# Three of four Strassen weight sums made by the DMA engines' adder on GpSimd's queue, and the pairs of a step in another order

## The chip, the cores and the metric

The kernel runs on one core of a Trainium2 chip. The metric is the device time of one execution in microseconds (us). Before the change it is 2227.79 us, the median of three runs (2227.02 to 2231.14). The engines named here are PE (TensorE, the matrix engine), DVE (VectorE), ACT (ScalarE), POOL (GpSimd) and SP (SyncE, which here only issues DMAs). The 16 DMA engines of the core are shared by all queues.

## The reference

One decoder layer on 256 tokens of width 2048, all in fp32. It holds two feed-forward layers (FFN), a mixer between them, and a per-layer embedding at the end:

```python
def swiglu(x, w_in, w_out):
    a, u = jnp.split(x @ w_in, 2, axis=-1)
    return (jax.nn.silu(a) * u) @ w_out

x = layer_norm(ALPHA * x + 0.5 * swiglu(x, ffn1_w_in[i], ffn1_w_out[i]), ln_g[i, 0], ln_b[i, 0])
...
x = layer_norm(ALPHA * x + merged @ mix_w_out[i], ln_g[i, 1], ln_b[i, 1])
x = layer_norm(ALPHA * x + 0.5 * swiglu(x, ffn2_w_in[i], ffn2_w_out[i]), ln_g[i, 2], ln_b[i, 2])
ple = jax.nn.sigmoid(x @ ple_w_gate[i]) * (p[i] @ ple_w_proj[i])
x = layer_norm(ALPHA * x + ple, ln_g[i, 3], ln_b[i, 3])
```

The hidden width D_FF is 5504. `x @ w_in` is the product that the change touches: it is [256, 2048] by [2048, 2 x 5504].

## The kernel before

**Passes.** To get nearly fp32 results from a faster matmul format, every operand is split into a high part (a cast) and a low part (operand less high part). A product of a 128-row block takes three matmuls of 128x128 by 128x512: high by high, high by low, low by high (L962, L963, L964).

**Weights.** Weights stream from HBM by SP's queue in pieces of two 128-row blocks by 512 columns (512 KB). ACT casts a piece to its high part `wh` (`weight_cast`, L897), DVE makes the low part `wl` (`weight_split`, L908). Such a piece, with what PE does with it, is called an element. Elements are used strictly in the order of the list `plan`. There are `NMAIN` = 6 slots for a `wh`/`wl` pair, so the cast of an element waits until PE has used up the one six places before it. Raw pieces have a ring of four buffers (`raw`); Strassen pieces have another ring of five (`sraw`).

**Strassen steps.** Chunks 2 to 10 of an FFN's columns are made by a `Quad`: the a half and the u half of a chunk, for both 128-token tiles, with part of the product done in Strassen's form. A Quad has two steps, and its pair of steps is followed by plain units on `w_out` (out units) for earlier chunks. There are nine Quads in each of two FFNs: 18 pairs, 36 steps. Each step loads four weight pieces k11, k12, k21, k22 into `sraw` and uses seven elements from them: 11, 22 and 21 as they are, and t1 to t4, which are sums. The sums are made in place, in the buffers that held the summands:

```python
"t1": dict(src=k11, add=k12, use=[("p5", "s1", lo)]),
"t3": dict(src=k12, add=k22, use=[("p7", "s3", lo)], free=[k12]),
"t2": dict(src=k11, add=k22, use=[("p6", "s2", lo)], drop=[k22]),
"t4": dict(src=k11, add=k21, use=[("p4", 1, hi)], drop=[k21], free=[k11]),
```

So t1, t2 and t4 follow one another in k11's buffer. `drop` gives a summand's buffer back after the sum, `free` gives the buffer back after the split; the pieces of the next step go into buffers so freed, in the order k12, k22, k21, k11. Four more elements (a0, a1, u0, u1) are plain raw pieces, each used for two products. The seven have one use (6 matmuls), the four have two (12 matmuls).

**What sets the order.** Whenever PE has used up an element, `feed` issues what it can, in this priority: a Strassen load, a raw load, a cast (with the sum in front of it on DVE, L891), a split. A scheduler then places the instructions of each engine in one fixed order, and inserts waits on semaphores; an engine runs its own list in order. The results of a Quad lie in seven PSUM banks p1 to p7; `after` combines them in the second step with DVE (L425) and ACT.

Of the kernel before, what the change touches and what calls it, by code (L numbers as in the profile page):

```python
# [14 lines left out]
ALU = mybir.AluOpType  # L15
# [15 lines left out]
LONG = (12, 4)  # L31
EXTRA = {"lead1": 3, "ffn1": 0, "tail1": 4, "hgrn": 0, "merge": 0, "lead2": 3, "ffn2": 0, "tail2": 4, "ple": 1}
NSRAW = 5
ALPHA = 2.0 ** 0.25
LN_EPS = 1e-5
RMS_EPS = 1e-6
# [30 lines left out]
class Quad:  # L67
# [11 lines left out]
    def __init__(self, stat, w, cols, width, after):  # L79
        self.stat, self.w, self.cols, self.width, self.after = stat, w, cols, width, after  # L80
        self.els = []
        for s in range(2):
            lo, hi = (2 * s, 2 * s + 1), (4 + 2 * s, 5 + 2 * s)
            n0, n1 = (8 + 4 * s, 9 + 4 * s), (10 + 4 * s, 11 + 4 * s)
            k11, k12, k21, k22 = ((self, s, n) for n in ("11", "12", "21", "22"))
            step = {
                "11": dict(src=k11, use=[("p1", 0, lo)]),
                "t1": dict(src=k11, add=k12, use=[("p5", "s1", lo)]),
                "22": dict(src=k22, use=[("p3", "s4", lo)]),
                "t3": dict(src=k12, add=k22, use=[("p7", "s3", lo)], free=[k12]),  # L90
                "t2": dict(src=k11, add=k22, use=[("p6", "s2", lo)], drop=[k22]),
                "21": dict(src=k21, use=[("p2", 0, hi)]),
                "t4": dict(src=k11, add=k21, use=[("p4", 1, hi)], drop=[k21], free=[k11]),
            }
            for n, ks in (("a0", n0), ("a1", n1)):
                step[n] = dict(load=[(ks, 0)], use=[("p2", 0, ks), ("p4", 1, ks)])
            for n, ks in (("u0", n0), ("u1", n1)):
                step[n] = dict(load=[(ks, 1)], use=[("p3", "d", ks), ("p5", 1, ks)])
            step["11"]["sums"] = [(k12, lo, 1), (k22, hi, 1), (k21, hi, 0), (k11, lo, 0)]
            order = "11 u0 t1 u1 22 t3 a0 t2 a1 21 t4".split()  # L100
            for n in order:
                self.els.append(dict(step[n], name=n, step=s))

# [2 lines left out]
def hybrid_layer(ctx: ExitStack, tc: tile.TileContext, x, p, ln_g, ln_b, ffn1_w_in, ffn1_w_out, mix_w_in,  # L106
                 conv_w, hg_lower_bound, hg_norm_w, branch_w_conv, branch_w_hgrn, mix_w_out,
                 ffn2_w_in, ffn2_w_out, ple_w_gate, ple_w_proj, out):
    nc = tc.nc
# [7 lines left out]
    op = pool("op", side="left")  # L117
# [111 lines left out]
    for b in (1, 2, 4, 8, 16, 32, 64):  # L229
        n = 64 // b  # L230
# [176 lines left out]
    def ffn(name, xs, w_in, w_out, ln_i, nxt):  # L407
        parts = [range(0, 2), range(2, 4), range(4, 6), range(6, 8), range(8, 11)]
        starts = [0, CC] + [DFF - (11 - ch) * CC for ch in range(2, 12)]
        gs = [Stat() for _ in parts]  # L410

        def turn(g, t, ci, h, w):
            defer(3, lambda: to_stat(g, t, ci, h, w // P, "g"))

        def in_units(ch, g, ci):
            c0 = starts[ch]
            w = starts[ch + 1] - c0
            if ch > 1:
                made = {}

                def work(tag):
                    return st.tile([P, CC], F32, tag=tag, name=tag, bufs=2 if tag == "silu" else 3)

                def both(o, a, b, op):
                    nc.vector.tensor_tensor(out=o, in0=a, in1=b, op=op)  # L425

                def after(el, ps):
                    if el["step"] == 0:
                        return
                    if el["name"] == "11":  # L430
                        made["c11"] = work("h")
                        nc.scalar.copy(made["c11"], ps["p1"])
                    elif el["name"] == "22":
                        made["c12"] = work("silu")
                        nc.scalar.copy(made["c12"], ps["p3"])
                        both(made["c12"], made["c12"], ps["p5"], ALU.add)
                    elif el["name"] == "t2":
                        made["e"], made["c22"] = work("silu"), work("h")
                        e = made["e"]
                        both(e, made["c11"], ps["p6"], ALU.add)  # L440
                        both(made["c12"], made["c12"], e, ALU.subtract)
                        both(e, e, ps["p7"], ALU.add)
                        both(made["c22"], ps["p5"], e, ALU.subtract)
                    elif el["name"] == "21":
                        h = made["c11"]
                        both(h, h, ps["p2"], ALU.add)
                        nc.scalar.activation(h, h, AF.Silu)
                        both(h, h, made["c12"], ALU.mult)
                        turn(g, 0, ci, h, CC)
                    elif el["name"] == "t4":  # L450
                        e = made["e"]
                        both(e, e, ps["p4"], ALU.add)
                        nc.scalar.activation(e, e, AF.Silu)
                        both(e, e, made["c22"], ALU.mult)
                        turn(g, 1, ci, e, CC)

                units.append(Quad(xs, w_in, (c0, DFF + c0), CC, after))
                return
            silu = {}

            def epi_a(t, acc):
                silu[t] = st.tile([P, CC], F32, tag="silu", name="silu", bufs=2)
                nc.scalar.activation(silu[t][:, :w], acc, AF.Silu)

            def epi_u(t, acc):
                h = st.tile([P, CC], F32, tag="h", name="h", bufs=3)
                nc.vector.tensor_tensor(out=h[:, :w], in0=silu[t][:, :w], in1=acc, op=ALU.mult)
                turn(g, t, ci, h, w)

            units.append(Unit(xs, w_in, 0, 16, c0, w, epi_a, split=(LONG if ln_i else EARLY) if ch == 0 else SPLIT))  # L470
            units.append(Unit(xs, w_in, 0, 16, DFF + c0, w, epi_u))

        def out_unit(pi, c):
            chunks, last = parts[pi], pi == len(parts) - 1
            row = starts[chunks[0]]
            nk = (starts[chunks[-1] + 1] - row) // P

            def epi_o(t, acc):
                settle(c)
                xc = xt[t][:, c * CC : (c + 1) * CC]  # L480
                if pi == 0:
                    nc.vector.scalar_tensor_tensor(out=xc, in0=xc, scalar=2.0 * ALPHA, in1=acc,
                                                   op0=ALU.mult, op1=ALU.add)
                else:
                    nc.vector.tensor_tensor(out=xc, in0=xc, in1=acc, op=ALU.add)
                if last:
                    ln_stat(t, c)
                    if c == 3:
                        layer_norm(t, ln_i, 0.5, nxt)

            units.append(Unit(gs[pi], w_out, row, nk, c * CC, CC, epi_o, split=(12,) if last and c == 3 else SPLIT))


        for pi, chunks in enumerate(parts):
            for ci, ch in enumerate(chunks):
                if ch == 1:
                    units.append(("ffn" + name, lambda: sums(xs)))
                in_units(ch, gs[pi], ci)
                if pi and ci < 2:
                    out_unit(pi - 1, 2 * ci)  # L500
                    out_unit(pi - 1, 2 * ci + 1)
        units.append(("tail" + name, lambda: None))
        for c in range(4):
            out_unit(len(parts) - 1, c)
# [325 lines left out]


    plan = []
    loads = {"raw": deque(), "sraw": deque()}
    for u in units:
        if isinstance(u, tuple):
            kind, n = u[0], EXTRA[u[0]]
            continue
        if isinstance(u, Quad):
            for el in u.els:
                for key, ks, n in el.get("sums", ()):  # L840
                    loads["sraw"].append((key, kind, u.w, ks[0] * P, 2, u.cols[n], u.width))
                if "load" in el:
# [35 lines left out]
    def drop(keys):  # L878
        for key in keys:
# [3 lines left out]
            else:  # L883
                held["freed"] += 1

    def weight_cast():
        el = plan[cur["cast"]]
        n, w, where = el["n"], el["w"], el["where"]
        raw = raws[el["src"]]
        if "add" in el:  # L890
            nc.vector.tensor_tensor(out=raw[:, :n, :w], in0=raw[:, :n, :w], in1=raws[el["add"]][:, :n, :w], op=ALU.add)  # L891
            drop(el.get("drop", ()))
        slots, bufs = (wp, NMAIN) if where == "main" else (region["pool"], EXTRA[where])
        h = slots.tile([P, KG, CC], F32R, tag="wh", name="wh", bufs=bufs)
        l = slots.tile([P, KG, CC], F32R, tag="wl", name="wl", bufs=bufs)
# [16 lines left out]
    def castable():  # L912
        i = cur["cast"]
        if i == len(plan) or i > cur["split"] + 1:
            return False
        el = plan[i]
        return (el["src"] in raws and el.get("add", el["src"]) in raws and room[el["where"]]
                and el["where"] in ("main", region["kind"]))

    def feed():  # L920
        while True:
            if may_load("sraw"):
                weight_dma("sraw")
            elif may_load("raw"):
                weight_dma()
            elif castable():
                weight_cast()
            elif cur["split"] < cur["cast"]:
# [119 lines left out]
```

## Time and profile before

| | before |
|---|---|
| median of 3 runs | 2227.79 us |
| the profiled execution | 2228.56 us |
| its span in the trace | 2226.7 us |
| granted PE clock, mean | 0.997 |
| read from HBM | 426.12 MB |

The profile is of one execution. Its page gives the busy time of each engine, the span in 40 slices, the DMA queues, the chain of work that ended last and the costliest groups of instructions. A group's row has the line of the kernel, engine, operation, the tiles written and read, their shape and the count, then the busy time in all and the mean in ns. A row of the timeline has start and duration in us, engine, line, operation, tiles and, in brackets, how long the engine had idled before it and what ended that. The rows themselves stand in the prediction, where they are used.

### The profile page before, as it was taken

Reading aid. Unit: us, or ns where it says so; the run is one execution under the profiler, and the core shown is the slowest. Engines: PE = TensorE matmul, PEld = TensorE weight load, DVE = VectorE, ACT = ScalarE, POOL = GpSimd, SP = SyncE. Lnnn points to the kernel's source line nnn. Section 1 sums busy time; section 2 is a strip of 40 time slices with the busy share of each in tenths; the row PEclk is TensorE's granted clock in tenths of the full one; section 3 lists DMA queues with packets and bytes.
Section 4 is the critical chain, followed back from the end, with each engine's and each line's share of the span. In section 5 each row is a group of like instructions: output and inputs, shape, how many; then the busy total and the mean of one; then the engine's idle time right before and its main releaser. Section 6 shows DMA issues by size and latency. Waiting matters only on the chain.

```text
span 2226.7 us, 26935 instructions
## 1 busy us (share of the span) xinstructions
PE 2203.0 (99%) x10110; PEld 1837.0 (82%) x10110; DVE 1685.6 (76%) x1952; ACT 1127.8 (51%) x1324; POOL 10.0 (0%) x32
## 2 busy tenths in 40 slices
PE   9999999999999999999999999999999999999997
PEld 7988888888887888888888888798888888888876
DVE  6788888888885678557555875769888888888668
ACT  5555555555555534434444443645555555555463
POOL 1000000000000000000000000000000000000000
PEclk9999999999999999999999999999999999999999
DMA  7666676566653665554555665567666556666564
GB/s 255 215 204 194 198 217 202 183 192 190 207 194 128 194 200 172 174 167 152 189 190 189 199 194 192 181 200 226 209 214 197 181 185 214 200 191 192 172 218 151
DMA packets 225334, 429.98 MB, mean 193 GB/s; under 512 B 13740, under 2 KB 22452, under 8 KB 225204
## 3 DMA queue, kind: packets, MB, share of 16 engines
q1 hardware_dynamic: 225204, 428.27, 60.6%
q8 instruction: 79, 1.29, 0.2%
q14 instruction: 51, 0.42, 0.1%
HBM read 426.12 MB, written 2.10 MB: 192 GB/s over the span
## 4 chain that ended last, share of the span: by engine, by line
PE 92%; DVE 4%; DMA 2%; ACT 1%; issue 1%; SPq 0%; DVEq 0%; ACTq 0%
PE bank L962 30%; PE bank L964 29%; PE bank L963 29%; DVE wl L908 2%; PE bank L243 2%; PE bank L600 1%; DVE sraw L891 1%; DMA raw<-in_ffn_w_in_dram 1%; ACT wh L897 0%; DMA sraw<-in_ffn_w_in_dram 0%; DMA gb<-in_ln_g_dram 0%; DMA x<-in_x_dram 0%; DMA raw<-in_ffn_w_out_dram 0%; DVE x L400 0%; DVE x L401 0%
## 5 line engine op out<-in xcount | busy, mean ns | idle before, releaser
L908 DVE TENSOR_TENSOR wl<-raw,wh 128x1024 fp32r<-128x1024 f32 (+2 forms) x660 | 788.6, 1203 | 262.8 <-ACT wh L897 245.4
L897 ACT CAST wh<-raw 128x1024 fp32r<-128x1024 f32 (+2 forms) x660 | 680.4, 1035 | 581.5 <-PE bank L964 410.1
L964 PE MATMUL bank<-wh,xl 128*128 128x512 f32 (+1 forms) x1736 | 670.9, 387 | 0.7 <-DVE xl L254 0.7
L963 PE MATMUL bank<-wl,xh 128*128 128x512 f32 (+1 forms) x1736 | 671.0, 387 | 0.0
L962 PE MATMUL bank<-wh,xh 128*128 128x512 f32 (+1 forms) x1736 | 669.6, 388 | 1.3 <-ACT xh L253 0.9
L897 ACT CAST wh<-sraw 128x1024 fp32r<-128x1024 f32 x252 | 262.5, 1050 | 273.1 <-PE bank L964 120.3
L908 DVE TENSOR_TENSOR wl<-sraw,wh 128x1024 fp32r<-128x1024 f32 x252 | 306.1, 1223 | 102.5 <-ACT wh L897 98.8
L964 PEld LDWEIGHTS bank<-wh,xl 128*128 128x128 f32 x1736 | 327.0, 188 | 64.5 <-DVE xl L254 2.4
L962 PEld LDWEIGHTS bank<-wh,xh 128*128 128x128 f32 x1736 | 327.1, 188 | 63.9 <-ACT xh L253 1.7
L963 PEld LDWEIGHTS bank<-wl,xh 128*128 128x128 f32 x1736 | 327.0, 188 | 61.8 <-DVE wl L908 0.2
L963 PE MATMUL bank<-wl,gh 128*128 128x512 f32 x880 | 343.9, 391 | 0.0
L964 PE MATMUL bank<-wh,gl 128*128 128x512 f32 x880 | 342.9, 391 | 0.0
L962 PE MATMUL bank<-wh,gh 128*128 128x512 f32 x880 | 341.9, 392 | 0.0
L964 PEld LDWEIGHTS bank<-wh,gl 128*128 128x128 f32 x880 | 165.4, 188 | 34.1
L962 PEld LDWEIGHTS bank<-wh,gh 128*128 128x128 f32 x880 | 165.3, 188 | 33.8
L963 PEld LDWEIGHTS bank<-wl,gh 128*128 128x128 f32 x880 | 165.4, 188 | 33.4
L891 DVE TENSOR_TENSOR sraw<-sraw 128x1024 f32<-128x1024 f32 x144 | 175.8, 1221 | 0.7
L964 PE MATMUL bank<-wh,sl 128*128 128x512 f32 x432 | 168.5, 390 | 0.0
L963 PE MATMUL bank<-wl,sh 128*128 128x512 f32 x432 | 168.4, 390 | 0.0
L962 PE MATMUL bank<-wh,sh 128*128 128x512 f32 x432 | 164.9, 390 | 0.5 <-ACT wh L897 0.5
L962 PEld LDWEIGHTS bank<-wh,sh 128*128 128x128 f32 x432 | 81.1, 188 | 17.9 <-ACT wh L897 1.4
L963 PEld LDWEIGHTS bank<-wl,sh 128*128 128x128 f32 x432 | 81.1, 188 | 16.9
(181 smaller groups left out, 1145.8 us busy)
## 6 DMA issues: line engine op xcount, KB each, us to landing
raw<-in_ffn_w_in_dram SPq DMA_DIRECT2D x176, 512.0 KB, 4.5
raw<-in_mix_w_in_dram SPq DMA_DIRECT2D x176, 512.0 KB, 4.6
raw<-in_ffn_w_out_dram SPq DMA_DIRECT2D x168, 512.0 KB, 4.9
sraw<-in_ffn_w_in_dram SPq DMA_DIRECT2D x144, 512.0 KB, 4.7
raw<-in_mix_w_out_dram SPq DMA_DIRECT2D x32, 512.0 KB, 5.4
raw<-in_ple_w_gate_dram SPq DMA_DIRECT2D x32, 512.0 KB, 4.9
raw<-in_ffn_w_in_dram SPq DMA_DIRECT2D x32, 384.0 KB, 4.0
raw<-in_branch_w_conv_dram SPq DMA_DIRECT2D x16, 512.0 KB, 4.9
```

Of the source, the lines that this page charges most:

```text
L243: state["turned"] = nc.tensor.transpose(tp[:, i * P : (i + 1) * P], src[:, i * P : (i + 1) * P], ident).ins
L600: nc.tensor.matmul(gp[:, (h * 2 + t) * 64 : (h * 2 + t + 1) * 64], kd[:, h, t * P : (t + 1) * P], qd[:, h, t, :], start=True, stop=True)
L891: nc.vector.tensor_tensor(out=raw[:, :n, :w], in0=raw[:, :n, :w], in1=raws[el["add"]][:, :n, :w], op=ALU.add)
L897: nc.scalar.copy(h[:, :n, :w], raw[:, :n, :w])
L908: nc.vector.tensor_tensor(out=l[:, :n, :w], in0=raw[:, :n, :w], in1=h[:, :n, :w].bitcast(F32), op=ALU.subtract)
L962: nc.tensor.matmul(acc, sh, wh[:, a, :n], start=first, stop=False)
L963: nc.tensor.matmul(acc, sh, wl[:, a, :n], start=False, stop=False)
L964: nc.tensor.matmul(acc, sl, wh[:, a, :n], start=False, stop=last)
```

## The change

The sums get a step of their own in `feed`, ahead of the cast. t1 stays on DVE. t2, t3 and t4 become DMAs with an adder, from one `sraw` buffer onto another, issued on GpSimd's queue. A sum is issued in the order of the list, when both summands are loaded and the split of an earlier element is issued (`behind`): of 11 for t1 and t3, of t1 for t2, of t2 for t4. The cast of a summed element now asks whether the sum has been issued. The order of a step's eleven elements changes, and two of the bank combinations in `after` hang on other elements.

```diff
+BY_DMA = ("t2", "t3", "t4")
...
-            order = "11 u0 t1 u1 22 t3 a0 t2 a1 21 t4".split()
+            order = "11 22 t1 21 u0 u1 t3 t2 a0 a1 t4".split()
+            for n, first in (("t1", "11"), ("t3", "11"), ("t2", "t1"), ("t4", "t2")):
+                step[n]["behind"] = len(order) * s + order.index(first)
...
-                    elif el["name"] == "22":
+                    elif el["name"] == "u1":
                         made["c12"] = work("silu")
...
-                    elif el["name"] == "21":
+                    elif el["name"] == "a1":
                         h = made["c11"]
...
+    def weight_add():
+        el = plan[adds.popleft()]
+        a, b = raws[el["src"]], raws[el["add"]]
+        if el["name"] in BY_DMA:
+            nc.gpsimd.dma_start(a, b, accum_op=ALU.add)
+        else:
+            nc.vector.tensor_tensor(out=a, in0=a, in1=b, op=ALU.add)
+        drop(el.get("drop", ()))
+        el["added"] = True
+
+    def addable():
+        if not adds:
+            return False
+        i = adds[0]
+        el = plan[i]
+        if el["src"] not in raws or el["add"] not in raws or cur["split"] <= el["behind"]:
+            return False
+        return el["name"] in BY_DMA or i <= cur["split"] + 1
...
     def weight_cast():
...
-        if "add" in el:
-            nc.vector.tensor_tensor(out=raw[:, :n, :w], in0=raw[:, :n, :w], in1=raws[el["add"]][:, :n, :w], op=ALU.add)
-            drop(el.get("drop", ()))
...
     def feed():
...
+            elif addable():
+                weight_add()
             elif castable():
```

What this does to DVE's list is seen at the start of a pair's second step. The number of an `sraw` tile tells which loaded piece it is. Before, 3447 is the second step's k11, 3117 its k12, 3375 its k22:

```order
L908 TENSOR_TENSOR wl_3459<-sraw_3447,wh_3458 128x1024 [waits DMAHW6_49,Activation_49]
L908 TENSOR_TENSOR wl_3475<-raw_3303,wh_3474 128x1024 [waits DMAHW0_49,Activation_49]
L891 TENSOR_TENSOR sraw_3447<-sraw_3447,sraw_3117 128x1024 [waits DVE_49]
L891 TENSOR_TENSOR sraw_3117<-sraw_3117,sraw_3375 128x1024 [waits DMAHW2_49,DVE_49]
L908 TENSOR_TENSOR wl_3488<-sraw_3447,wh_3487 128x1024 [waits Activation_49]
L908 TENSOR_TENSOR wl_3504<-raw_3352,wh_3503 128x1024 [waits DMAHW1_49,Activation_49]
L891 TENSOR_TENSOR sraw_3447<-sraw_3447,sraw_3375 128x1024 [waits DVE_49]
```

Now 3402 is the second step's k11, 3342 its k22, 3111 its k12, 3389 its k21 (a split is now L934, a sum on DVE L902):

```order
L934 TENSOR_TENSOR wl_3459<-sraw_3402,wh_3458 128x1024 [waits DMAHW6_49,Activation_49]
L934 TENSOR_TENSOR wl_3471<-sraw_3342,wh_3470 128x1024 [waits DMAHW1_49,Activation_49]
L902 TENSOR_TENSOR sraw_3402<-sraw_3402,sraw_3111 128x1024 [waits DVE_49]
L934 TENSOR_TENSOR wl_3481<-sraw_3402,wh_3480 128x1024 [waits Activation_49]
L934 TENSOR_TENSOR wl_3500<-sraw_3389,wh_3499 128x1024 [waits DMAHW3_49,Activation_49]
L934 TENSOR_TENSOR wl_3516<-raw_3364,wh_3515 128x1024 [waits DMAHW0_49,Activation_49]
L934 TENSOR_TENSOR wl_3528<-raw_3376,wh_3527 128x1024 [waits DMAHW2_49,Activation_49]
L934 TENSOR_TENSOR wl_3540<-sraw_3111,wh_3539 128x1024 [waits DMASW1_49,PE_49,Activation_49]
L934 TENSOR_TENSOR wl_3554<-sraw_3402,wh_3553 128x1024 [waits DMASW2_49,Activation_49]
```

Of the step's sums only t1 is left on DVE (36 in the whole program, where there were 144), and the splits of t3 and t2 (the last two rows) wait for semaphores of GpSimd's DMAs (DMASW).

POOL's list had nothing at this place. It now has the sums of all steps, one behind the other; 3069 and 3054 are the first step's k11 and k21:

```order
L900 DMA sraw_3069<-sraw_2996 128x1024 [waits DMASW5_49,DMASW0_49,DVE_49]
L900 DMA sraw_3069<-sraw_3054 128x1024 [waits DMAHW3_49,DMASW7_49,DVE_49]
L900 DMA sraw_3111<-sraw_3342 128x1024 [waits DMAHW7_49,DMAHW1_49,DVE_49]
L900 DMA sraw_3402<-sraw_3342 128x1024 [waits DMASW3_49,DMASW0_49,DVE_49]
L900 DMA sraw_3402<-sraw_3389 128x1024 [waits DMAHW3_49,DMASW2_49,DVE_49]
```

These are t2 and t4 of the first step, then t3, t2 and t4 of the second. Each t2 and t4 waits for the sum before it in the same buffer (DMASW) and for a split on DVE.

SP's list of loads at the same place, before:

```order
L868 DMA sraw_3375<-in_ffn1_w_in_dram 128x2x512 [waits DVE_49]
L868 DMA sraw_3406<-in_ffn1_w_in_dram 128x2x512 [waits DVE_49]
L868 DMA raw_3388<-in_ffn1_w_in_dram 128x2x512 [waits DMAHW6_49,DVE_49]
L868 DMA raw_3419<-in_ffn1_w_in_dram 128x2x512 [waits DMAHW7_49,DVE_49]
L868 DMA sraw_3447<-in_ffn1_w_in_dram 128x2x512 [waits DVE_49]
L868 DMA sraw_3450<-in_ffn1_w_in_dram 128x2x512 [waits DVE_49]
```

and now:

```order
L877 DMA sraw_3342<-in_ffn1_w_in_dram 128x2x512 [waits DMASW7_49,DMASW6_49]
L877 DMA raw_3376<-in_ffn1_w_in_dram 128x2x512 [waits DMAHW5_49,DVE_49]
L877 DMA sraw_3389<-in_ffn1_w_in_dram 128x2x512 [waits DVE_49]
L877 DMA raw_3414<-in_ffn1_w_in_dram 128x2x512 [waits DMAHW6_49,DVE_49]
L877 DMA raw_3426<-in_ffn1_w_in_dram 128x2x512 [waits DMAHW7_49,DVE_49]
L877 DMA sraw_3402<-in_ffn1_w_in_dram 128x2x512 [waits DMASW0_49]
L877 DMA sraw_3444<-in_ffn1_w_in_dram 128x2x512 [waits DVE_49]
```

Every Strassen load waited for DVE; now those of k22 (3342) and k11 (3402) wait for DMA sums of the step before, because these read or write the buffer that the load fills.

More of the change, by code (lines that the diff above doesn't have):

```diff
@@ L832, in hybrid_layer @@
     plan = []
+    adds = deque()
     loads = {"raw": deque(), "sraw": deque()}
@@ L838, in hybrid_layer @@
         if isinstance(u, Quad):
+            base = len(plan)
             for el in u.els:
+                if "add" in el:
+                    adds.append(len(plan))
+                    el["behind"] += base
                 for key, ks, n in el.get("sums", ()):
@@ L916, in castable @@
         el = plan[i]
-        return (el["src"] in raws and el.get("add", el["src"]) in raws and room[el["where"]]
+        return (el["src"] in raws and ("add" not in el or el.get("added")) and room[el["where"]]
                 and el["where"] in ("main", region["kind"]))
```

## The prediction

> **What bounds the kernel now.** I read the page's busy times first, then the slices, then who TensorE (PE) waits for, then single steps in the timeline.
>
> ```profile
> span 2226.7 us, 26935 instructions
> PE 2203.0 (99%) x10110; PEld 1837.0 (82%) x10110; DVE 1685.6 (76%) x1952; ACT 1127.8 (51%) x1324; POOL 10.0 (0%) x32
> PE   9999999999999999999999999999999999999997
> DVE  6788888888885678557555875769888888888668
> PEclk9999999999999999999999999999999999999999
> ```
>
> PE is busy for 99% of the span at full clock. VectorE (DVE) is at eight or nine tenths where the Strassen steps run (slices 2 to 12 and 26 to 36), but a high share is no bound by itself. A busy PE is also no proof that it runs at its own rate, so the waits come next, and then the distance between matmuls.
>
> ```profile
> PE bank L962 <- ACT wh L897: 0.5, 2, 0.3
> ...
> PEld bank L962 <- ACT wh L897: 1.4, 2, 0.7
> ...
> PEld bank L963 <- DVE wl L908: 0.2, 1, 0.2
> ...
> 289.06 0.39 PE L962 MATMUL bank<-wh,xh 128*128 128x512 f32 x1
> 289.29 0.39 PE L963 MATMUL bank<-wl,xh 128*128 128x512 f32 x1
> 289.51 0.39 PE L964 MATMUL bank<-wh,xl 128*128 128x512 f32 x1
> 289.74 0.39 PE L962 MATMUL bank<-wh,xh 128*128 128x512 f32 x1
> ```
>
> The first three rows (us in total, times, longest) are all of the waits for prepared weights in the whole run, PE's own and those of its weight loads: about 2 us. The starts in the timeline lie 0.227 us apart (289.74 less 289.06, by three), although one matmul is drawn 0.39 us long; they overlap. A step has 7 elements with one use and 4 with two, so 7 x 6 + 4 x 12 = 90 matmuls, 20.40 us. The windows of one pair's two steps confirm it.
>
> ```profile
> 278.42:298.82 20.40, 20.40 (x92) 16.90 (x91) 15.03 (x14) 8.99 (x9) 0.00 (x0) 1.00 0.64 188
> 298.82:319.22 20.40, 20.40 (x92) 16.91 (x91) 20.37 (x21) 13.42 (x15) 0.00 (x0) 1.00 0.75 234
> ```
>
> The columns are PE, PEld, DVE, ACT and POOL busy, then clock, DMA share and GB/s. PE holds its rate even in the second step, where DVE is busy for 20.37 of 20.40 us. So weights are made just in time, and PE has nothing to gain from a freer DVE beyond a us or two. What matters is whether the weights still come in time.
>
> **The change part by part.** *DVE sums removed.*
>
> ```profile
> L891 DVE TENSOR_TENSOR sraw<-sraw 128x1024 f32<-128x1024 f32 x144 | 175.8, 1221 | 0.7
> ```
>
> Of 144 sums, 36 (t1) stay on DVE and 108 go: 108 x 1.221 = 132 us of DVE time. It all lies beside PE work, so I count its gain at 0; the waits above bound it at 2 us.
>
> *The moved pairs and epilogue steps.* The same 90 matmuls, casts, splits and bank sums are issued in another order. Cover for the moved epilogues is PE's own work: they read banks that are finished, and none is used again before the next unit. Cost 0, and about one 0.69 us bank sum per pair (18 x 0.7 = 12 us) if that cover went.
>
> *The DMA sums.* How long one takes from issue to landing (call it A) is in no row of before. The nearest rows:
>
> ```profile
> L868 SPq DMA_DIRECT2D sraw<-in_ffn_w_in_dram x144: 367/368/450, 35.9 to 2012.9; - x144
> DMA to landing us min/median/max: 3.6/4.7/7.0
> ...
> L402 SPq DMA_DIRECT2D out_dram<-x x8: 332/332/348, 2212.7 to 2223.2; - x8
> DMA to landing us min/median/max: 2.2/2.3/2.4
> ...
> q1 hardware_dynamic: 225204, 428.27, 60.6%
> ```
>
> A load of the same 512 KB lands in 4.7 us. By the queue's row, a packet takes 0.606 x 16 x 2226.7 / 225204 = 0.096 us on an engine, and a load has 256 packets over 16 engines: 1.53 us is moving, the rest latency and queueing. A sum has two operands, so I let it move twice as much: 4.7 + 1.53 = 6.2 us. Lower end: the 256 KB store, whose source is on the chip as here, takes 2.3 us, of which 0.77 is moving; with 3.07 of moving that is 4.6 us. Upper end: two loads one after the other, 9.4 us.
>
> Now the room. These rows are from the first step above, which starts at 278.42:
>
> ```profile
> 282.50 1.05 ACT L897 CAST wh<-sraw 128x1024 fp32r<-128x1024 f32 x1 [1.67 <-PE bank L964]
> ...
> 293.45 1.05 ACT L897 CAST wh<-sraw 128x1024 fp32r<-128x1024 f32 x1 [4.45 <-DMA sraw<-in_ffn_w_in_dram]
> ...
> 294.53 1.23 DVE L908 TENSOR_TENSOR wl<-sraw,wh 128x1024 fp32r<-128x1024 f32 x1 [4.27 <-ACT wh L897]
> 295.67 1.22 DVE L908 TENSOR_TENSOR wl<-raw,wh 128x1024 fp32r<-128x1024 f32 x1
> ...
> 288.93 1.72 SPq L868 DMA_DIRECT2D sraw<-in_ffn_w_in_dram  x2
> ```
>
> The cast at 282.50 is t2, eighth in the list before. It begins when PE finishes the second, u0 (278.42 + 1.36 + 2.72 = 282.50): with six slots a cast cannot begin before the element six places ahead is used up. The load at 288.93 is k11 of the second step; its cast begins at 293.45, its split at 294.53, and splits follow at 1.14 us. A cast and its split together cost about 2.4 us. In the old order PE needs that element at 298.82, so there were 3 us to spare.
>
> In the new order three DMA sums stand in one chain through each pair. From the start of the first step:
> - the second element, 22, is used up at 2.72, so t2 can be cast; split by 5.1;
> - only then can t4's sum go out (it overwrites the buffer that this split reads): 5.1 + A;
> - only then is the k21 buffer free for the second step's k11: load 4.7, so 9.8 + A; SP stands at this load meanwhile, and behind it are loads for elements at least four places on;
> - cast and split of 11, split of 22, t1's sum and its cast and split: 2.4 + 1.14 + 1.14 + 2.4, so 16.9 + A;
> - t2's sum, cast, split: 19.3 + 2A. On POOL it stands behind t3's sum, which went out 2.4 us earlier and still has up to 0.7 us to move;
> - t4's sum, cast, split: 21.7 + 3A, or 22.4 + 3A with that 0.7.
>
> PE wants the low half of this t4 at 20.40 + 19.04 + 0.23 = 39.67 (the ten elements before it take 19.04). So the room for three sums is 39.67 - 22.4 = 17.3 us, 5.8 each. At A = 6.2 it is missed by 1.3 us a pair. There are 18 pairs (nine chunks, two layers of FFN); between them lie plain out units, and the first step of a pair has them as cover, so the miss is paid once a pair: 18 x 1.3 = 23 us.
>
> *The DMA engines.* The second step already moves 234 GB/s at a share of 0.75. Three sums add 3 x 3.07 = 9.2 us of all 16 engines to 0.75 x 20.4 = 15.3: 24.5 us of work in 20.4. Some slides into the out units, but the DMAs of this chain will queue. A load waits 1.1 us at the shares of before (4.7 less the least, 3.6). I add half of that again, 0.5 us, to each of the four DMAs of the chain; 0 and 1.1 are the ends. The miss becomes 1.3 + 4 x 0.5 = 3.3 us a pair, **18 x 3.3 = 59 us**.
>
> **Two rules of the Trainium skill.** The row of the sums: DVE is busy 20.37 of 20.40 us with fp32 operations of two operands. "SBUF — State Buffer", section "SBUF: two separate sides", says that a DMA issued on GpSimd has its descriptors written by GpSimd, and that DVE can lock it out while it runs in its two-port mode. The page names copies for that mode, not sums of two operands, so by its letter nothing is added here; no run here shows it yet. "DMA: Bandwidth & Descriptors", section "Anatomy of one DMA — SWDGE (gpsimd) path", fits 2.0 us plus bytes at 436 GB/s; an estimate from it for twice 512 KB is 4.4 us a sum, which is under the room of 5.8. The Trainium skill's lock is the third rival below, its fit speaks for the first.
>
> **The rivals.**
> 1. *The sums stay hidden: no change.* At the lower end A is 4.6 us, with the 0.5 of queueing 5.1. Then three sums and the added load delay take 3 x 5.1 + 0.5 = 15.8 of the 17.3, and PE waits for nothing: 2227 to 2230. It decides at 5.8 us (5.6 with the slower load). For it: a sum's operands are on the chip, like the store's. Against: the store ran with empty queues at the end. Its cousin, a faster kernel, has at most the 2 us of above. The Trainium skill's fit, above, points here. Chance 0.28, with 0.03 more for faster.
> 2. *DMA engines become the bound.* Behind the two steps above come out units, whose window is:
>
> ```profile
> 319.22:341.00 21.78, 21.78 (x101) 18.04 (x100) 17.40 (x20) 11.01 (x13) 0.00 (x0) 1.00 0.58 185
> ```
>
>    In these 62.6 us the engines work 0.64 x 20.4 + 0.75 x 20.4 + 0.58 x 21.8 = 41.0 now. Six sums fit if one takes at most (62.6 - 41.0) / 6 = 3.6 us of all engines; that is where this rival decides. At 3.07 it doesn't. If an addition passes at half the speed of moving, a sum takes 6.1, and 41.0 + 36.8 = 77.8 us of work make each pair 15 us longer: 270 us, about 2500. Against it: nothing shows that adding is slower than moving. Chance 0.12.
> 3. *DVE holds the issue up.* If every sum's issue waits out one DVE operation, 1.22 us, the miss grows by 3 x 1.22 = 3.7 a pair, 66 us: 2354. For it: DVE leaves hardly a gap in the second step. Against: 132 us of DVE work are gone. The Trainium skill's lock, above, would be its mechanism. Chance 0.10.
>
> **How the numbers follow.** Forecast: the profiled execution took 2228.6 us (span 2226.7 and 1.9 around it; the median of the runs shown is 0.8 lower), plus 59 is 2288. Its chance is 0.47, for anything between 2233 and 2340. Alone it runs from A = 6.2 without queueing (2252) to each of four DMAs later by 1.1 (2331). The range has to take in no change, so it begins at 2226; it ends at 2425, where the upper end of A lies ((3 x 9.4 - 17.3) x 18 = 196 us more), and leaves out most of the second and the faster case. A measurement of this kernel tells about 0.2% (4.5 us) from no change. Slower: 0.47 + 0.12 + 0.10 = 0.69; same 0.28; faster 0.03.
>
> **What would show it.** On the page of the changed kernel DVE should lose 132 us, and a second DMA queue should carry 108 sums. Right: their time to landing is 6 to 7.5 us, PE shows gaps of 2 to 5 us once a pair, at t4 of its second step, with the cast of a summed tile waiting for a DMA. Under 5.6 us and no such waits: rival one. DMA share at nine tenths or more through the pairs: rival two. Landing well above 7.5 with idle engines, issue late on POOL: rival three. I would be wrong altogether if t2's split were not what t4's sum waits for, or if PE waited in the first steps as well.

## The result and the profile after

| | before | after |
|---|---|---|
| median | 2228.51 us (4 runs, 2227.02 to 2231.14) | 2349.07 us (4 runs, 2347.20 to 2351.55) |
| ratio | 1 | 1.054, 95% interval 1.0522 to 1.0559 |
| span of the profiled execution | 2226.7 us | 2346.6 us |
| mean granted PE clock | 0.997 | 0.988 |

The kernel became 120.6 us slower. The page of the profile after, its busy times, three of its slice rows and the queue of the sums:

```profile
span 2346.6 us, 27184 instructions
PE 2249.8 (96%) x10110; PEld 1840.5 (78%) x10110; DVE 1557.1 (66%) x1844; ACT 1112.0 (47%) x1323; POOL 101.6 (4%) x140
DVE  6567666767666568557545875767766676766667
PEclk9999999999999999999999999999999999999999
DMA  7787887787775564554565565578787878877565
q0 software_dynamic: 15552, 56.63, 13.1%
```

DVE lost 128.5 us (132 were expected), 108 sums went to a second DMA queue, and PE's share fell from 99% to 96%. One sum takes 0.131 x 2346.6 / 108 = 2.85 us of all 16 engines (3.07 were expected). Who waited for weights, from the view of the waits (us in total, times, longest):

```profile
ACT wh L923 <- DMA sraw<-sraw: 344.7, 92, 9.1
PEld bank L990 <- ACT wh L923: 95.3, 85, 4.0
PE bank L990 <- ACT wh L923: 63.0, 80, 3.6
PEld bank L991 <- DVE wl L934: 15.7, 25, 1.6
```

PE's waits for weights were about 2 us in all before. Now casts on ACT stand for DMA sums, and PE stands for the casts. The same pair as in the prediction (it now starts at 298.14), in windows with the columns used there; the second row is its second step, the third the out units after it:

```profile
298.14:318.54 20.40, 20.40 (x91) 16.89 (x90) 10.06 (x10) 8.17 (x8) 0.84 (x1) 1.00 0.90 258
318.54:344.04 25.50, 22.29 (x93) 17.06 (x91) 15.65 (x16) 12.81 (x15) 2.55 (x3) 0.99 0.79 208
344.04:367.82 23.78, 23.78 (x103) 19.45 (x103) 20.59 (x25) 12.28 (x14) 1.70 (x2) 0.94 0.72 218
```

The first step keeps its 20.40 us; the second takes 25.50 instead of 20.40, the out units 23.78 instead of 21.78, at a clock of 0.94. The DMA engines are at nine tenths only in the first step. ACT's timeline of this pair shows the chain:

```profile
301.81 1.05 ACT L923 CAST wh<-sraw 128x1024 fp32r<-128x1024 f32 x1 [1.01 <-DMA sraw<-sraw]
...
312.46 1.05 ACT L923 CAST wh<-sraw 128x1024 fp32r<-128x1024 f32 x1 [7.63 <-DMA sraw<-sraw]
...
320.87 1.99 ACT L923 CAST wh<-sraw 128x1024 fp32r<-128x1024 f32 x2 [2.69 <-DVE sraw L902]
...
329.00 1.05 ACT L923 CAST wh<-sraw 128x1024 fp32r<-128x1024 f32 x1 [2.25 <-DMA sraw<-sraw]
...
340.08 1.04 ACT L923 CAST wh<-sraw 128x1024 fp32r<-128x1024 f32 x1 [7.66 <-DMA sraw<-sraw]
341.03 3.88 ACT L923 CAST wh<-raw 128x1024 fp32r<-128x1024 f32 x4
...
341.18 0.50 PE L990 MATMUL bank<-wh,xh 128*128 128x512 f32 x1 [1.77 <-ACT wh L923]
342.13 0.73 PE L990 MATMUL bank<-wh,gh 128*128 128x512 f32 x2 [0.45 <-ACT wh L923]
```

The casts are t2 and t4 of the first step, then t1, t2 and t4 of the second. ACT stands 7.63 and 7.66 us for the two t4 sums. When the last has come, four casts of the out units follow at once, 0.95 us each, and PE waits for them too (342.13).

### The profile page after: what moved, and what is told of

It reads as the page before. It is cut to its first block, busy times and chain, and to the rows that moved or that the text cites. A ratio compares the mean times of both kernels' runs of the same rounds, so it can differ in the third digit from the quotient of the medians.

```text
span 2346.6 us, 27184 instructions
## 1 busy us (share of the span) xinstructions
PE 2249.8 (96%) x10110; PEld 1840.5 (78%) x10110; DVE 1557.1 (66%) x1844; ACT 1112.0 (47%) x1323; POOL 101.6 (4%) x140
## 3 DMA queue, kind: packets, MB, share of 16 engines
q8 instruction: 79, 1.29, 0.2%
## 5 line engine op out<-in xcount | busy, mean ns | idle before, releaser
L934 DVE TENSOR_TENSOR wl<-raw,wh 128x1024 fp32r<-128x1024 f32 (+2 forms) x660 | 781.6, 1203 | 252.0 <-ACT wh L923 236.6
L923 ACT CAST wh<-raw 128x1024 fp32r<-128x1024 f32 (+2 forms) x660 | 670.5, 1033 | 529.1 <-PE bank L992 352.9
L990 PE MATMUL bank<-wh,xh 128*128 128x512 f32 (+1 forms) x1736 | 676.0, 392 | 39.7 <-ACT wh L923 38.1
L934 DVE TENSOR_TENSOR wl<-sraw,wh 128x1024 fp32r<-128x1024 f32 x252 | 304.6, 1224 | 371.8 <-ACT wh L923 369.6
L990 PE MATMUL bank<-wh,sh 128*128 128x512 f32 x432 | 171.5, 397 | 13.9 <-ACT wh L923 13.8
L900 POOL DMA_DIRECT2D sraw<-sraw x108 | 91.8, 850 | 1694.0 <-DVE sraw L902 817.4
```

What stands on the lines that cost most here:

```text
L900: nc.gpsimd.dma_start(a, b, accum_op=ALU.add)
L923: nc.scalar.copy(h[:, :n, :w], raw[:, :n, :w])
L934: nc.vector.tensor_tensor(out=l[:, :n, :w], in0=raw[:, :n, :w], in1=h[:, :n, :w].bitcast(F32), op=ALU.subtract)
L990: nc.tensor.matmul(acc, sh, wh[:, a, :n], start=first, stop=False)
```

## The experiments

Theory: a pair has one chain, first-step t4, k11 load, second-step t1, t2, t4; its sums by DMA are longer than its room, and what comes in late is PE's loss. Rivals: the new order alone costs; the volume of the sums costs (engines as the bound); GpSimd's issue costs; each t4 sum costs by itself, wherever it stands.

The distance between the starts of neighbouring matmuls shows where PE lost time: each distance over 0.24 us, less 0.227, summed up, gives 25 us before and 143 after, a difference of 118 beside 119.9 in the span. The sums by place below are of this kind.

**Order alone.** All sums stay on DVE, in the new order.

```diff
-BY_DMA = ("t2", "t3", "t4")
+BY_DMA = ()
```

> The new order and the new place of the sums, but all four sums on DVE (108 sums of 1.22 us come back to it). Chain theory (the loss is three DMA sums in one chain through each pair, of which t4's is the longest): no DMA sum, so no loss, 2228 to 2233, and PE waits for prepared weights under 5 us in all. Rival, overloaded DMA engines: also 2228 to 2233. Rival, the new order or the moved bank sums cost by themselves: 2240 or more, with PE waits in the pairs.

Measured: 2233.43, ratio 1.0034 (1.0018 to 1.0050): 5.7 us slower. Its waits stand almost all in the first two pairs of the second FFN. The order is a small part of the loss, not nothing.

**t2 and t3 alone, t4 alone.** Two kernels.

```diff
-BY_DMA = ("t2", "t3", "t4")
+BY_DMA = ("t2", "t3")      # first kernel
+BY_DMA = ("t4",)           # second kernel
```

> t4 back on DVE, t2 and t3 by DMA. Chain theory: only t2's sum of the second step (5.9 us) is left in the chain; it ends some 10 us early, so 2228 to 2235. Rival, overloaded DMA engines, with a loss by the number of sums: two thirds of 121 us, about 2309.

> Only t4 by DMA, t2 and t3 on DVE. Chain theory: 22.1 us of other work and two sums; at 8.4 us each (as in the change) 38.9 of 39.67 us, so it just fits, 2228 to 2240, with PE waits at t4 of single pairs at most. If t4's sum is faster here, since no load stands behind a DMA sum of t2 and is released with it, it takes 5 to 7 us, and no PE wait is left. Rival, overloaded DMA engines: a third of 121 us, about 2269.

Measured: 2234.17 with t2 and t3 by DMA, ratio 1.0028 (1.0014 to 1.0041), as the order alone; 2306.69 with t4 alone, ratio 1.0355 (1.0325 to 1.0385), far over its expectation. The last row of each kernel's view of the sums' line, first t2 and t3, then t4, tells why:

```profile
DMA to landing us min/median/max: 4.5/4.8/6.0
```

```profile
DMA to landing us min/median/max: 5.8/7.3/9.3
```

So 72 sums by DMA cost nothing beyond the order, and the volume is no bound; a t4 sum alone takes 7.3 us and costs. Fitted over the 108 sums of the changed kernel, the time from a sum's issue to its last packet is 4.50 us plus 0.90 for each 512 KB of loads started meanwhile (correlation 0.97). With fewer than half a load its median is 4.39 (71 sums), with more than 2.5 it is 7.69 (33 sums). The semaphore that tells of the landing comes 0.3 to 0.5 us later, at 4.8 and 8.1. The t4 sums are the ones that meet loads, 3.5 of them in the median; t3 meets none and t2 0.1.

The expectation for t4 alone failed in its other work. The second step's t4 was split at 42.3 us from the pair's start (median of 18 pairs), not at 38.9. The splits of that step's t1 and t2 lie 6.8 us apart there, and as far with all sums on DVE, because DVE splits 21, u0, u1 and t3 in between. With t2's sum by DMA they lie 8.1 apart, so that sum adds only 1.3 us to the chain.

**The early k11 load.** The load that stands behind t4's sum in the chain is put ahead of it.

```diff
-step["11"]["sums"] = [(k12, lo, 1), (k22, hi, 1), (k21, hi, 0), (k11, lo, 0)]
+step["11"]["sums"] = [(k12, lo, 1), (k11, lo, 0), (k22, hi, 1), (k21, hi, 0)]
```

> All three sums by DMA as in the change, but the pieces of a step are loaded in the order k12, k11, k22, k21. So the next step's k11 goes into the buffer that t2's sum frees, not into the one that t4's sum frees, and only k21, which is needed two elements later, waits for t4's sum. Chain theory: the first step's t4 sum and the load behind it leave the chain (12 us of it), the second step's t4 is ready some 3 us before PE wants it, 2228 to 2240. Rival, overloaded DMA engines: the same bytes move and the same sums queue, so 2320 to 2350.

Measured: 2298.34, ratio 1.0318 (1.0278 to 1.0358). Better by 51 us, but a miss: ACT's timeline in one pair shows that the chain only lost its load.

```profile
504.28 2.95 ACT L923 CAST wh<-sraw 128x1024 fp32r<-128x1024 f32 x3 [7.51 <-DMA sraw<-sraw]
510.11 2.00 ACT L923 CAST wh<-sraw 128x1024 fp32r<-128x1024 f32 x2 [2.88 <-DVE sraw L902]
...
518.23 1.05 ACT L923 CAST wh<-sraw 128x1024 fp32r<-128x1024 f32 x1 [1.77 <-DMA sraw<-sraw]
...
529.44 1.04 ACT L923 CAST wh<-sraw 128x1024 fp32r<-128x1024 f32 x1 [7.78 <-DMA sraw<-sraw]
```

The three casts at 504.28 are t4, 11 and 22. Element 11 had its data and still stood 7.51 us behind t4's cast, since ACT casts in order. A wait at the head of an in-order engine holds back everything behind it, ready or not.

**The first step's t4 used later.** k11 early, and the first step's t4 is cast and used behind 21 of the second step.

```diff
+order = [(0, n) for n in "11 22 t1 21 u0 u1 t3 t2 a0 a1".split()]
+order += [(1, n) for n in "11 22 t1 21 u0 u1 t3 t2 a0 a1 t4".split()]
+order.insert(order.index((1, "21")) + 1, (0, "t4"))
...
```

> All three sums by DMA, k11 loaded early as in e2, and besides the first step's t4 is cast and used four elements later, behind 21 of the second step, so that ACT does not stand at it while the second step's 11, 22 and t1 could be cast. Chain theory: what is left in the chain of a pair is t2's sum (5.9) and t4's sum (8.3) of the second step; t4 is ready at 36 of 39.67 us, so no loss but that of the order alone (5.7 us in e1): 2228 to 2237. Rival, overloaded DMA engines: the bytes and sums are the same, 2290 or more.

Measured: 2289.07, ratio 1.0277 (1.0248 to 1.0305), a miss again. PE's waits at the second step's t4 fell from 29.0 us (36.7 with only k11 early) to 5.3, but 21.5 us of waits stayed in the out units and 9.5 at 21. PE's transposes (L251) also waited 16.6 us for the moved epilogue's results on DVE.

**The same with the second step's t4 on DVE.** This asks whether those waits of the out units are the trace of a t4 that comes with no lookahead left.

```diff
+def by_dma(el):
+    return el["name"] in BY_DMA and (el["name"], el["step"]) != ("t4", 1)
...
```

> The second step's k11 loaded early and the first step's t4 used after 21 of the second step (as in the run with the late t4, 2289), and the second step's t4 back on DVE. Theory (what was left there is a second-step t4 that lands with no lookahead to spare, so that the casts of the out units come one by one): the out units' waits of 21.5 us go, about 10 us at 21 stay: 2240 to 2260. Rival (the out units' waits come from the order, or from the first step's t4): no more than 10 us better, 2280 or over.

Measured: 2243.17, ratio 1.0074 (1.0044 to 1.0103), as expected. The out units' waits went from 21.5 to 2.6 us and those of the transposes for the epilogue from 16.6 to 1.4; those at 21 stayed (11.8). So what PE loses in the out units comes from the second step's t4 sum, even where PE hardly waits at t4 itself.

**One t4 sum of the two.** t2 and t3 stay with the DMA engines in both steps; t4 only in the second, or only in the first (`by_dma` as above, with step 0 or 1).

> Only the first step's t4 goes back to DVE; t2 and t3 of both steps and the second step's t4 stay with the DMA engines, 90 sums. Theory (one chain through the pair, with a fixed amount of room): without the first step's t4 sum the chain is about 8 us shorter, the second step's t4 is split about 36 to 37 us from the pair's start where PE wants it at 39.67, and nothing in the pair waits: 2230 to 2245, about what the order alone gave (2233). Rival (each t4 sum delays its own cast and costs by itself): half of the loss with both t4 sums stays, 2280 to 2300.

> Only the second step's t4 goes back to DVE; the first step's t4 stays with the DMA engines with t2 and t3 of both steps, 90 sums. Theory (one chain): t1 of the second step, whose buffer the first step's t4 sum holds up, is split at about 25.5 us where PE wants it at 23.35, so PE waits about 2 us a pair in the second step at 11, t1 or 21, and the low end of the chain, t4, comes in time: 18 x 2 = 36 us and some 5 for the order, 2255 to 2285. Rival (each t4 sum costs by itself): half of the loss with both, 2280 to 2300, with its waits in the first step at t4.

Measured: 2279.54 and 2279.52, ratio 1.0237 each (1.0207 to 1.0267). The second figure is inside the chain's range and at the rival's edge; its waits stand at t1 and 21 of the second step (14.1 and 12.2 us), where the chain puts them, and hardly at the first step's t4 (2.6). The first is a miss for the chain, at the rival's edge. Medians of 18 pairs, counted from the pair's start, show why.

| us from the pair's start | both t4 | first only | second only | order alone |
|---|---|---|---|---|
| t4 of step 1 cast | 14.7 | 14.2 | 8.6 | 8.5 |
| 11 of step 2 cast | 18.6 | 18.2 | 14.2 | 13.9 |
| t1 of step 2 split | 25.5 | 25.2 | 21.2 | 20.9 |
| t2 of step 2 split | 33.6 | 33.5 | 29.5 | 27.7 |
| t4 of step 2 split | 44.6 | 38.1 | 40.1 | 32.4 |

With only the second sum, t4 is ready at 40.1, not at 36 to 37: freed of the first sum, the k11 load goes out 6 us sooner but then takes 5.5 us instead of 3.8, and the sum at the end still takes its 8. So t4 comes just as PE gets there (39.44), with no lookahead left, and the loss is taken behind it. Part of it looks different, in the waits of this kernel:

```profile
PE bank L993 <- ACT wh L926: 11.2, 17, 1.5
...
PE bank L994 <- DVE wl L937: 9.0, 16, 1.5
...
PE bank L247 <- DVE h L429: 13.9, 15, 1.3
```

The last row is the moved epilogue: its bank sums on DVE come late, and PE's transposes (L247) wait for them, 13.9 us. The prediction counted on this cover and priced its loss at 12 us; it held in the changed kernel and failed here. The two halves lose 46 us each beyond the order alone (75 us of distances in each, 29 with the order), both together 114, more than the sum: sums in one chain add up before PE waits. But a t4 sum at the end of a pair costs by itself too, so the rival is not wrong about that one. Why the epilogue is late in this kernel and not in the changed one was not tried.

**Copy instead of sum.** The operands are moved and not added.

```diff
-nc.gpsimd.dma_start(a, b, accum_op=ALU.add)
+nc.gpsimd.dma_start(a, b)
```

> The three DMAs copy the summand over the buffer in place of adding to it (the sums t2, t3 and t4 are left out). What the adder costs: a copy reads one operand where a sum reads two. If a sum's moving time is that of reading twice, an undisturbed one (t3's) lands in 4.4 - 1.4 = 3.0 us, t4's in 6 to 6.9, and the kernel takes 2280 to 2310. Rival, the adder's arithmetic or GpSimd's issue is the cost: landings and time stay within 0.3 us and 15 us of those of the change (2349).

Measured: 2253.49 (one run), lower than expected. The queue's row and the landing:

```profile
q0 software_dynamic: 15552, 56.63, 6.2%
```

```profile
DMA to landing us min/median/max: 2.8/2.9/8.6
```

The same packets take 0.062 x 2251.8 / 108 = 1.29 us of 16 engines instead of 2.85, and an undisturbed copy is done 1.67 us sooner (t3: 2.54 against 4.21, counted from issue to the last packet). As many DMAs issued in the same places by GpSimd cost 26 us instead of 120; what a sum has over a copy is the rest. A small part of that is GpSimd's issue, which takes 0.53 us for a copy and 0.85 for a sum. For the copies the same fit is 2.60 us plus 1.20 a load. The Trainium skill, "Collectives: The Full Stack", section "The bandwidth ceiling: the fold count and why AG ≠ RS ≠ AR", says of a ReduceScatter that its add pays for two source reads and not for its arithmetic; the factor of 2.2 here (2.85 over 1.29) agrees in size, and no run here separates the read from the addition.

**Fewer bytes in the loads.** The raw loads of a0, a1, u0 and u1 are halved.

```diff
-loads["raw"].append((len(plan), kind, u.w, ks[0] * P, 2, u.cols[n], u.width))
+loads["raw"].append((len(plan), kind, u.w, ks[0] * P, 1, u.cols[n], u.width))
...
```

> All as in the change, but the raw pieces of a Strassen step (a0, a1, u0, u1) are loaded by half, one of two blocks, which is used for both (half of these weights is left out). If t4's sum is long because it shares the DMA engines with the loads in flight (0.9 us for each 512 KB, by the changed kernel's trace), it now meets about 2.5 loads' worth in place of 3.5: it lands 0.7 to 1.3 us earlier, and the kernel gains 25 to 55 us: 2295 to 2325. Rival, t4's sum is long by itself (its third place in one buffer, its late issue): it lands as before within 0.3 us, 2335 to 2350.

Measured: 2327.03 (one run), at the slow end of what was expected. A t4 sum met 2.9 loads of 512 KB instead of 3.5 and its last packet came 0.94 us sooner (medians, 6.69 against 7.63), and the kernel gained 22 us. The loads beside the sum are a cause of its length.

## Why the prediction was right or wrong

**Right: direction, range and the chain; wrong in size.** The forecast was 2288 in 2226 to 2425; measured are 2349, a loss of 120.6 us where 59 was forecast. Of the signs that it named, these came: 108 sums on a second queue, gaps at t4 of the second step, a cast that stands for a DMA. The landing of 6 to 7.5 us did not: the median of all sums is 5.4, which is half of rival one's sign (under 5.6), with 4.5 for t3 and 8.1 for t4. PE also waited in the first steps, which was named as a sign against it, but only for 5.7 us in all, at t4.

**Right almost to the end: the chain.** It put the split of the second step's t4 at 43.0 us from the pair's start (22.4 + 3 x 6.2 and four times 0.5); the median is 44.6. That it came so near is luck in part, since single terms were off and made up for each other: t2's split 6.0 instead of 5.1, first-step t4 at 14.7 instead of 11.8, the k11 load 3.8 instead of 5.2, and from t1's split to t2's 8.1 instead of the 9.8 put down.

**Wrong in size: the queueing of 0.5 us "to each of the four DMAs of the chain".** It is not spread. The undisturbed sum lands in 4.5 us (t3), close to the lower end (4.6). The k11 load's 3.8 is near the least of before (3.6), and the second step's t2 takes 0.9 us more than t3, about the 0.7 that the prediction gave it behind t3's sum. Each t4 sum takes 8.1 from issue to landing; it meets 3.5 loads at 0.90 us each. A mean wait of before's loads could not show that: what counts is which loads are released in the same place.

**Wrong: "between them lie plain out units, and the first step of a pair has them as cover, so the miss is paid once a pair".** This is the step that failed; it priced all that comes behind t4 at 0. Before and after by place (the fourth row holds the distances under 0.6 us where the clock was halved, the others all the rest):

| us beyond 0.227 between matmuls | before | after | forecast, added |
|---|---|---|---|
| inside the pairs | 1.6 | 74.9 | 59 |
| in the out units | 3.4 | 30.3 | 0 |
| other places, transposes among them | 18.4 | 18.4 | 0 |
| matmuls at half clock | 1.6 | 19.7 | 0 |
| all | 25.0 | 143.3 | 59 |

Inside the pairs the loss is 4.1 us a pair where 3.3 was forecast. It does not stand where it was put: 29 us are at t4 of the second step, some 30 at its t1 and 21, 8 at its 11, because the first t4 sum delays the start of the chain too. Behind the pair ACT has cast nothing of the out units while it stood at t4; casts then come at 0.95 us and PE eats them as they come, which costs 27 us. The experiments with the late t4 show it: with the second t4 back on DVE those waits go. The halved clock is a further price of the waits, up to 18 us. So of some 59 us beyond the forecast, 14 are waits inside the pairs, 27 waits in the out units and 18 the clock.

**Nearly right: the order, priced at 0.** It costs 5.7 us alone.

**The rivals.** *Hidden*: its lower end of A was the true one for an undisturbed sum, and with t2 and t3 alone it is what happens; the Trainium skill's fit ("DMA: Bandwidth & Descriptors", section "Anatomy of one DMA — SWDGE (gpsimd) path"), by which a sum was estimated at 4.4 us, agrees in size with the landing of sums without loads beside them (t3: 4.5) and not with that of the t4 sums (8.1). *Engines as the bound*: 0.90 in one step of the pair and 0.79 in the next, 2.85 us a sum, and 72 sums that cost nothing; it is no bound, though the load on the engines lengthens the t4 sums. *DVE holds the issue up*: the issues take 0.84 to 1.01 us and begin soon after the split that they wait for. From the view of the sums' line (issue in ns, min/median/max, then the landing):

```profile
L900 POOL DMA_DIRECT2D sraw<-sraw x108: 841/854/1005, 86.9 to 2146.4; - x108
...
DMA to landing us min/median/max: 4.5/5.4/9.3
```

The lock of "SBUF — State Buffer", section "SBUF: two separate sides", which the Trainium skill names for copies, is not seen with these sums and splits: 87 of the 108 issues had DVE busy for over 80% of them and took 0.848 us in the mean, the 18 with DVE almost idle 0.854.

## What to carry to other kernels

Price a DMA by the transfers that are released with it, at its place in the order, not by a mean over the run. When work leaves an engine with slack for a path with more latency, follow the chain of buffers that it frees and the in-order engine that waits at its head: what stands behind that wait is late as well, and the lookahead lost there is paid again in the next stage. A resource at 76% whose removal buys nothing is no reason to move work off it.

## What the runs showed of the hardware

A DMA that adds costs 2.85 us of 16 engines for 512 KB, 2.2 times the copy (1.29), and lands in 4.5 us undisturbed, the copy in 2.9.

PE's clock halves after a wait of under 2 us. In the pair above, windows (same columns) around the wait of 1.77 us:

```profile
339.98:343.39 3.41, 1.77 (x6) 1.24 (x7) 2.23 (x3) 3.31 (x4) 0.00 (x0) 1.00 0.62 190
```

```profile
343.39:346.82 3.43, 3.43 (x9) 2.47 (x8) 3.43 (x4) 1.53 (x2) 0.00 (x0) 0.50 0.80 188
```

```profile
343.39 0.62 PE L991 MATMUL bank<-wl,xh 128*128 128x512 f32 x1
343.81 0.63 PE L992 MATMUL bank<-wh,xl 128*128 128x512 f32 x1
344.24 0.73 PE L991 MATMUL bank<-wl,gh 128*128 128x512 f32 x1
```

After 3.41 us in which PE was busy for 1.77, the next 3.43 us run at 0.50, with matmuls 0.43 us apart instead of 0.227. The trace after has 13 stretches at half clock, that of before two, with the idle end of the run among them in each. The Trainium skill, "TensorE: Matmul & The Clock Gate", section "What's actually happening", gives a window of 3413 ns, which agrees in length, and halves the clock after an idle window; here only four idle gaps of PE were over 2 us, so by these rows a window that is not wholly idle can be enough. Cut into windows of this length, the trace after shows half clock behind every full-clock window in which PE was busy for less than 0.47 of it, and behind none over 0.54. Of seven windows between, two stayed at full clock. What decides there was not tried.
